# x^T and the first weight piece in shared transfers, and causal attention on two pairs of heads at a time

## The chip, the cores and the metric

The program runs on one NeuronCore of a Trainium2 chip. The metric is the device time of one execution in microseconds (us), from repeated runs of the same program; lower is better. Engines are named as the profile names them: PE is TensorE (PEld its weight loads), DVE is VectorE, ACT is ScalarE, POOL is GpSimd, SP is SyncE, which only starts DMA transfers here.

## What is computed

One layer of a decoder trunk on 256 tokens of width 1024, all in float32. The normed input goes through one projection `w_in`, whose columns feed four token mixers and their gates; the mixers are projected, gated, summed, projected once more, and a SwiGLU FFN follows. The part that matters here:

```python
h = rmsnorm(x, norm_mix)
proj = h @ w_in                       # m_z, m_xbc, m_dt, b_qkv, c_qkv, c_f, d_q, d_kv, gate_logits
y_a = mamba2_branch(...)              # A: state space scan, 8 heads
y_b = moba_attention(...)             # B: causal attention, 8 heads of 64, bias by distance
y_c = forgetting_attention(...)       # C: causal attention, 8 heads of 64, cumulative forget gates
y_d = sliding_window_attention(...)   # D: window 128, 8 query heads on 2 key heads, sinks
merged = sum(sigmoid(gate_i) * (y_i @ w_branch_i))
x = x + merged @ w_out
x = x + (silu(h2 @ w_ffn_gate) * (h2 @ w_ffn_up)) @ w_ffn_down       # h2 = rmsnorm(x, norm_ffn)
out = rmsnorm(x, norm_final)
```

With 256 tokens every attention branch is, for each head, a lower triangle of 256 by 256: 128 x 128 scores for the first half of the queries, 128 x 256 for the second.

## The kernel before, in words

**Precision.** A float32 product is made of three fast products: each operand is split into a rounded high part and the rest (`hi` and `lo`), and PE computes hi*hi, hi*lo and lo*hi. ACT makes the high parts (L331), DVE the low parts (L339).

**The weight stream.** The weights come from HBM in pieces of 1 MB, in the order of `stream()`, through three raw buffers (`fetch`, L323), all issued by SP. A piece is asked for when the low part of the piece three places ahead of it is done. The in-projection pieces come first (`xbc0`, `xbc1`, `n0`, `qkB0`, `vB0` and so on), then for the branches in the order A, B, D, C four gate pieces and two branch pieces each (PE groups `pg` at L989 and `pb`), then the out-projection `wo`, the FFN's `gu` and `dn`.

**The head.** The first piece is not fetched like the others. x^T (x transposed, 1 MB in two tiles `xT0`, `xT1`) and the piece `xbc0` (1 MB) come in six chunks of the 8 blocks of 128 rows, one transfer of x^T and one of the weights per chunk, at L395 and L397: 12 transfers, 11 of them from SP and the first of the weights from POOL, with the constants `chan` (the norm weights) between them on SP (L399). For each chunk ACT scales x^T into the high part of `xx` (L431) and makes the weights' high part (L432), DVE the two low parts (L434, L436), and PE adds the chunk's products (L440, six matmuls of 256 columns per block of 128 rows, 48 in all). Every later projection reads `xx`. Eight matmuls on constants (L424) run on PE before the first chunk. Behind the head, `xbc1` and `n0` follow on PE with no other work between; the norm's factor r comes later, from x itself (`xn`).

**Attention, woven in.** All other work of the mixers is written as generators (`att_pair`, `ssd_pair`, `conv` and others) that yield a `Need` of estimated engine time and of buffers. The `Weaver` holds clocks of PE, DVE and ACT, which are estimates, and between groups of projection matmuls (`wv.tick`) runs those stages whose inputs it takes to be ready and whose buffers are free. The order of all instructions on each engine is thus fixed when the program is built. What a stage needs before it is put on PE is (L764 and around):

```python
yield Need(pe=680, att=2)      # two PSUM banks of the five of tag att
```

One call of `att_pair` handles one pair of heads: the scores (`s`, L764 and L766, operands of 64 rows, one head in the upper and one in the lower half of PE's array), then on DVE the bias, negation and row minimum (L777, L779), on ACT the exponential (L783, L784), on DVE the division by the row sums (L801, L802), on PE six transposes (`pt`, L809), on ACT the copy (L815), on PE the products with the values (`y`, in `pv`, L685 and L687, outputs of 64 columns), and the split of y into parts. There are four pairs in each of B, C and D. The state space branch ends in `pv` too (`ya`). Rows of the bias tables come by POOL's DMA queue (`rows2`, L584).

Of the kernel before, what the change touches and what calls it, by code (L numbers as in the profile page):

```python
# [199 lines left out]
def hybrid_block_kernel(ctx: ExitStack, tc: tile.TileContext, A, out):  # L200
# [28 lines left out]

    def acc(name, shape=(128, 512)):  # L230
# [80 lines left out]
    for n in names:  # L311
# [72 lines left out]
    act.activation(early, early, AF.Exp)  # L384
    chan = const("chan", [128, 64])
    rows = const("rows", [128, 32])
# [41 lines left out]
    hb, lb, wb = (cut(t, 8, 256) for t in (h0, l0, w0))  # L428
    for a, b in chunks:
        for k in range(a, b):  # L430
            act.activation(xx(k)[:, 0, :], xT[k // 4][:, k % 4, :], AF.Copy, scale=nm_mix[:, k : k + 1])  # L431
        act.activation(hb[:, a:b, :], wb[:, a:b, :], AF.Copy)  # L432
        for k in range(a, b):
            dve.scalar_tensor_tensor(xx(k)[:, 1, :], xT[k // 4][:, k % 4, :], nm_mix[:, k : k + 1],  # L434
                                     xx(k)[:, 0, :].bitcast(F32), ALU.mult, ALU.subtract)
        dve.tensor_tensor(lb[:, a:b, :], wb[:, a:b, :], hb[:, a:b, :].bitcast(F32), ALU.subtract)  # L436
# [316 lines left out]
    def att_pair(br, j, heads, load_rows, q, k, vs, addend, sinks=None):  # L753
        yield Need(rows=1)
        rw = load_rows()
        yield Need()
        yield Need(pe=680, att=2)
        if j == 0:
            new_y(br)
        sts = []  # L760
        hs = [slice(64 * i, 64 * i + 64) for i in range(2)]
        ss = [att("s%s%d" % (br, heads[i]), [128, 384]) for i in range(2)]
        for i in range(2):
            pe.matmul(ss[i][:, 0:128], q[hs[i], 0:128], k[hs[i], 0:128], start=True, stop=True)  # L764
        for i in range(2):
# [560 lines left out]
```

## Time and profile before

| | |
|---|---|
| time, median of 3 runs | 521.33 us (520.48 to 521.71) |
| the profiled execution: its own time, its span | 519.55 us, 517.8 us |
| PE, DVE, ACT busy in the span | 98%, 68%, 55% |
| HBM read over the span | 94.46 MB |
| mean granted TensorE clock | 0.994 of full |

A line of the profile's timeline gives the start, the time taken, the engine, the source line, and the tiles written and read. Matmuls of a stream overlap in the pipeline: what one costs is the distance from its start to the next one's, not the duration shown. A float32 matmul that is not split shows as two records.

### The profile page before, as it was taken

Reading aid. Unit: us, or ns where it says so; the run is one execution under the profiler, and the core shown is the slowest. Engines: PE = TensorE matmul, PEld = TensorE weight load, DVE = VectorE, ACT = ScalarE, POOL = GpSimd, SP = SyncE. Lnnn points to the kernel's source line nnn. Section 1 sums busy time; section 2 is a strip of 40 time slices with the busy share of each in tenths; the row PEclk is TensorE's granted clock in tenths of the full one; section 3 lists DMA queues with packets and bytes.
Section 4 is the critical chain, followed back from the end, with each engine's and each line's share of the span. In section 5 each row is a group of like instructions: output and inputs, shape, how many; then the busy total and the mean of one; then the engine's idle time right before and its main releaser. Section 6 shows DMA issues by size and latency. Waiting matters only on the chain.

```text
span 517.8 us, 7989 instructions
## 1 busy us (share of the span) xinstructions
PE 507.6 (98%) x3106; PEld 444.1 (86%) x3106; DVE 350.6 (68%) x658; ACT 284.1 (55%) x511; POOL 29.7 (6%) x61
## 2 busy tenths in 40 slices
PE   7999999999999999999999999999999999999995
PEld 6998998987897778888888899998888888888884
DVE  4577778898896947547386494688676676673435
ACT  6667464567575863443444363876655655543412
POOL 2008110012110000000000000000000000000001
PEclk8999999999999999999999999999999999999998
DMA  7974464465355244727537283355545555585302
GB/s 230 388 277 173 162 217 150 156 217 192 137 177 183 82 164 162 250 92 280 191 128 278 89 332 148 97 229 177 219 173 172 215 184 169 210 313 181 144 0 82
DMA packets 17122, 96.06 MB, mean 186 GB/s; under 512 B 2235, under 2 KB 3563, under 8 KB 6844
## 3 DMA queue, kind: packets, MB, share of 16 engines
q1 hardware_dynamic: 15660, 91.15, 48.8%
q0 software_dynamic: 1424, 4.41, 3.1%
q8 instruction: 24, 0.39, 0.3%
q14 instruction: 14, 0.11, 0.1%
HBM read 94.46 MB, written 1.09 MB: 185 GB/s over the span
## 4 chain that ended last, share of the span: by engine, by line
PE 95%; issue 2%; DMA 1%; ACT 1%; DVE 1%; SPq 0%; POOL 0%; POOLq 0%; ACTq 0%; DVEq 0%
PE pg L989 17%; PE gu L260 13%; PE pd L1186 11%; PE pb L250 8%; PE gu L262 7%; PE pvC L989 2%; PE pvB L989 2%; PE qkC L252 2%; PE po L250 1%; PE gu L250 1%; PE gu L253 1%; PE po L253 1%; PE gu L252 1%; PE qkC L250 1%; PE po L252 1%
## 5 line engine op out<-in xcount | busy, mean ns | idle before, releaser
L260 PE MATMUL gu<-x3x,hi_gu 128*128 128x512 f32 x288 | 72.1, 392 | 0.0
L989 PE MATMUL pg<-hi_g,xx 128*128 128x512 f32 x256 | 64.3, 393 | 0.0
L260 PEld LDWEIGHTS gu<-x3x,hi_gu 128*128 128x128 f32 x288 | 51.8, 189 | 9.3
L989 PEld LDWEIGHTS pg<-hi_g,xx 128*128 128x128 f32 x256 | 47.4, 188 | 11.1 <-issue 1.5
L339 DVE TENSOR_TENSOR lo_gu<-raw_gu,hi_gu 128x1024 fp32r<-128x1024 f32 x44 | 53.2, 1216 | 1.4 <-ACT hi_gu L331 1.4
L331 ACT ACTIVATE hi_g<-raw_g 128x1024 fp32r<-128x1024 f32 x32 | 32.9, 1053 | 29.0 <-DMA raw_g<-in_w_dram 14.2
L331 ACT ACTIVATE hi_gu<-raw_gu 128x1024 fp32r<-128x1024 f32 x44 | 45.6, 1051 | 1.5 <-PE gu L253 1.5
L1186 PE MATMUL pd<-hi_dn,aa 128*128 128x512 f32 (+1 forms) x176 | 46.2, 384 | 0.0
L339 DVE TENSOR_TENSOR lo_g<-raw_g,hi_g 128x1024 fp32r<-128x1024 f32 x32 | 38.1, 1219 | 8.8 <-ACT hi_g L331 8.8
L262 PEld LDWEIGHTS gu<-x3x,lo_gu 128*128 128x128 f32 x288 | 39.3, 190 | 2.8
L339 DVE TENSOR_TENSOR lo_dn<-raw_dn,hi_dn 128x1024 fp32r<-128x1024 f32 x22 | 26.1, 1220 | 21.6 <-ACT hi_dn L331 21.5
L262 PE MATMUL gu<-x3x,lo_gu 128*128 128x256 f32 x288 | 40.2, 282 | 0.0
L1186 PEld LDWEIGHTS pd<-hi_dn,aa 128*128 128x128 f32 x176 | 32.6, 188 | 6.5
L331 ACT ACTIVATE hi_dn<-raw_dn 128x1024 fp32r<-128x1024 f32 x22 | 22.4, 1052 | 25.3 <-PE pd L1186 25.3
L1128 DVE TENSOR_TENSOR gs<-gu,ge 128x256 f32<-128x256 f32 x36 | 15.3, 424 | 30.7 <-ACT ge L1127 30.6
L989 PE MATMUL pg<-lo_g,xx 128*128 128x512 f32 x128 | 34.3, 389 | 0.0
L1127 ACT ACTIVATE ge<-gu 128x256 f32<-128x256 f32 x36 | 13.5, 374 | 27.5 <-PE gu L262 27.3
L989 PEld LDWEIGHTS pg<-lo_g,xx 128*128 128x128 f32 x128 | 24.0, 188 | 5.1
L1186 PE MATMUL pd<-lo_dn,aa 128*128 128x512 f32 (+1 forms) x88 | 26.7, 384 | 0.0
L339 DVE TENSOR_TENSOR lo_wb<-raw_wb,hi_wb 128x1024 fp32r<-128x1024 f32 x16 | 19.3, 1220 | 9.3 <-ACT hi_wb L331 9.3
L913 ACT ACTIVATE gate<-pg,r1h 128x512 f32<-128x512 f32 x16 | 11.0, 687 | 25.7 <-PE pg L989 25.7
L929 DVE SCALAR_TENSOR_TENSOR gp<-gate,pb 128x512 f32<-128x512 f32 x12 | 8.2, 687 | 21.2 <-PE pb L250 20.9
(326 smaller groups left out, 1140.5 us busy)
## 6 DMA issues: line engine op xcount, KB each, us to landing
raw_gu<-in_w_dram SPq DMA_DIRECT2D x22, 1024.0 KB, 4.8
raw_g<-in_w_dram SPq DMA_DIRECT2D x16, 1024.0 KB, 4.8
raw_dn<-in_w_dram SPq DMA_DIRECT2D x11, 1024.0 KB, 4.8
raw_wb<-in_w_dram SPq DMA_DIRECT2D x8, 1024.0 KB, 4.9
raw_qkB<-in_w_dram SPq DMA_DIRECT2D x4, 1024.0 KB, 5.0
raw_qkC<-in_w_dram SPq DMA_DIRECT2D x4, 1024.0 KB, 4.9
raw_wo<-in_w_dram SPq DMA_DIRECT2D x4, 1024.0 KB, 4.8
raw_vB<-in_w_dram SPq DMA_DIRECT2D x2, 1024.0 KB, 8.8
```

Of the source, the lines that this page charges most:

```text
L250: pe.matmul(o, l, r, start=start, stop=stop)
L252: pe.matmul(o, l, r[:, 0, :], start=start, stop=False)
L253: pe.matmul(o, l, r[:, 1, :], start=False, stop=stop)
L260: pe.matmul(o, wh(k), x(k), start=start and i == 0, stop=False)
L262: pe.matmul(o[:, 0, :], wl(k), x(k)[:, 0, :], start=False, stop=stop and i == n - 1)
L331: act.activation(parts[name][0][:, s], raws[name][:, s], AF.Copy)
L339: dve.tensor_tensor(lo[:, s], raws[name][:, s], hi[:, s].bitcast(F32), ALU.subtract)
L913: act.activation(gates[b, t][:, 512 * nh : 512 * nh + 512], p, AF.Tanh, scale=r1h[:, t : t + 1])
L989: pe.matmul(pg[t], l, r, start=kh == 0 and i == 0, stop=kh == 1 and i == len(terms) - 1)
L1127: act.activation(e[:, j, :], p[j][:, 1, :], AF.Copy)
L1128: dve.tensor_tensor(s[:, j, :], p[j][:, 0, :], e[:, j, :], ALU.add)
L1186: pe.matmul(o, l, r, start=start and j == 0, stop=stop and j == len(terms) - 1)
```

## The change

Two independent edits. First, x^T and the weights of `xbc0` lie side by side in one array in HBM (`head`: per block of 128 rows, 256 columns of x^T, then 256 of weights), which the host builds; they come into four tiles `hd` in five transfers, of which ACT's queue issues the second and SP the others. `chan` moves from SP to ACT's queue, POOL issues no part of the head, and the raw buffer that `xbc0` had is free from the start. Second, `att_pair` becomes `att_quad`, which handles two pairs of heads: the scores of both pairs in a row, then DVE and ACT work pair by pair, transposes pair by pair, then the products with the values of both pairs in a row. A quad reserves its buffers `pp`, `sm` and `pt` for four heads (`hold`), and asks for four of the five PSUM banks of tag `att` at its start. Which instructions there are hardly changes; their order does.

```diff
     chan = const("chan", [128, 64])
+    act.dma_start(chan, A["chan"])
...
-    xT = [slot("xT%d" % i) for i in range(2)]
-    w0 = wp.tile([128, WMAX], F32, tag="raw", name="raw_xbc0", bufs=3)
-    raws["xbc0"] = w0
-    chunks = ((0, 1), (1, 2), (2, 4), (4, 6), (6, 7), (7, 8))
+    hd = [slot("hd%d" % i, (128, 2, 2, 256)) for i in range(4)]
+    chunks = ((0, 1), (1, 2), (2, 4), (4, 6), (6, 8))
     for a, b in chunks:
-        nc.sync.dma_start(xT[a // 4][:, a % 4 : (b - 1) % 4 + 1, :], A["xT"][:, a:b, :])
-        src = bass.AP(tensor=A["w"].tensor, offset=woff["xbc0"] + 256 * a, ap=[[2048, 128], [1, 256 * (b - a)]])
-        (nc.sync if a else pool).dma_start(w0[:, 256 * a : 256 * b], src)
-        if a == 0:
-            nc.sync.dma_start(chan, A["chan"])
+        (act if a == 1 else nc.sync).dma_start(hd[a // 2][:, a % 2 : (b - 1) % 2 + 1, :, :], A["head"][:, a:b, :, :])
+    act.activation(early, early, AF.Exp)
...
-    def att_pair(br, j, heads, load_rows, q, k, vs, addend, sinks=None):
-        yield Need(rows=1)
-        rw = load_rows()
+    def att_quad(br, pairs, addend, sinks=None):
+        rws = []
+        for _, _, load_rows, _, _, _ in pairs:
+            yield Need(rows=1)
+            rws.append(load_rows())
         yield Need()
-        yield Need(pe=680, att=2)
-        if j == 0:
+        yield Need(pe=1360, att=4, pp=4, sm=4)
+        hold(pp=4, sm=4)
+        if pairs[0][0] == 0:
             new_y(br)
...
+        for ss, (_, _, _, q, k, _) in zip(sss, pairs):
+            for i in range(2):
+                pe.matmul(ss[i][:, 0:128], q[hs[i], 0:128], k[hs[i], 0:128], start=True, stop=True)
+        for ss, (_, _, _, q, k, _) in zip(sss, pairs):
+            for i in range(2):
+                pe.matmul(ss[i][:, 128:384], q[hs[i], 128:256], k[hs[i], 0:256], start=True, stop=True)
...
+        yield Need(pe=1300, att=2)
+        ys = [att("y%s%d" % (br, p[0]), [128, 256]) for p in pairs]
+        for y, sts, p in zip(ys, stss, pairs):
+            pv(y, p[5], sts)
+            rel(pt=2)
...
-    for j in range(4):
-        wv.later(lambda j=j: moba_pair(j), ["qkB%d" % j, "vB0", "vB1", "erow"], True)
+    for js in ((0, 1), (2, 3)):
+        wv.later(lambda js=js: moba_quad(js), ["qkB%d" % j for j in js] + ["vB0", "vB1", "erow"], True)
...
-    a["w"] = np.concatenate([pk(ps[n]) for n in stream()])
+    a["w"] = np.concatenate([pk(ps[n]) for n in stream()[1:]])
+    a["head"] = np.stack([a["xT"], pk(ps[stream()[0]]).reshape(128, 8, 256)], 2)
```

The queue of SP at the program's start, before (`xT` and `raw_xbc0` are the head, sizes in partitions x elements; `raw_xbc1` and `raw_n0`, the next two pieces, stand right behind these rows):

```order
L395 DMA xT0_81<-in_xT_dram 128x256
L399 DMA chan_79<-in_chan_dram 128x64
L395 DMA xT0_81<-in_xT_dram 128x256
L397 DMA raw_xbc0_83<-in_w_dram 128x256
L395 DMA xT0_81<-in_xT_dram 128x512
L397 DMA raw_xbc0_83<-in_w_dram 128x512
L395 DMA xT1_82<-in_xT_dram 128x512
L397 DMA raw_xbc0_83<-in_w_dram 128x512
L395 DMA xT1_82<-in_xT_dram 128x256
L397 DMA raw_xbc0_83<-in_w_dram 128x256
L395 DMA xT1_82<-in_xT_dram 128x256
L397 DMA raw_xbc0_83<-in_w_dram 128x256
```

and with the change:

```order
L399 DMA hd0_81<-in_head_dram 128x512
L399 DMA hd1_82<-in_head_dram 128x1024
L399 DMA hd2_83<-in_head_dram 128x1024
L399 DMA hd3_84<-in_head_dram 128x1024
L328 DMA raw_xbc1_91<-in_w_dram 128x512 x4
L328 DMA raw_n0_96<-in_w_dram 128x2176
```

Twelve transfers stood ahead of `raw_xbc1` on SP, now four; `chan` and the second half of `hd0` stand on ACT's queue, ahead of all its other work.

On PE, the values' products of the first pair of branch B stood before next to the scores of the second, between the projection pieces `xbc3` and `z0`:

```order
L250 MATMUL xbc3_763<-xx3_119,lo_xbc3_609 128x256 x2
L685 MATMUL yB0_850<-ptsB0_846,vB_565 64x256
L685 MATMUL yB0_850<-ptsB1_848,vB_565 64x256
L687 MATMUL yB0_850<-ptsB0_846,vB_565 64x128
L687 MATMUL yB0_850<-ptsB1_848,vB_565 64x128
L764 MATMUL sB2_858<-qkB0_438 128x128
L764 MATMUL sB3_859<-qkB0_438 128x128
L766 MATMUL sB2_858<-qkB0_438 128x256
L766 MATMUL sB3_859<-qkB0_438 128x256
L252 MATMUL z0_864<-xx0_116,hi_z0_697 128x256
```

With the change the scores of all four heads stand in that place, and the products of both pairs follow later, in the middle of `qD0`:

```order
L255 MATMUL xbc3_721<-xx3_113,lo_xbc3_601 128x256 x2
L772 MATMUL sB0_803<-qkB0_430 128x128
L772 MATMUL sB1_804<-qkB0_430 128x128
L772 MATMUL sB2_805<-qkB0_430 128x128
L772 MATMUL sB3_806<-qkB0_430 128x128
L775 MATMUL sB0_803<-qkB0_430 128x256
L775 MATMUL sB1_804<-qkB0_430 128x256
L775 MATMUL sB2_805<-qkB0_430 128x256
L775 MATMUL sB3_806<-qkB0_430 128x256
L257 MATMUL z0_815<-xx0_110,hi_z0_679 128x256
```

The scores of the first pair moved back from `qkB1` to this place, and 12 runs of scores in the program became 6.

The end of the attention work moved too. Before, the last products of branch C (`yC3`) were on PE ahead of the first branch projection `pb000`. With the change the last quad begins only ahead of the third branch's projection, and its end stands 24 gate matmuls ahead of the matmuls that read it:

```order
L689 MATMUL yC3_3017<-ptsC6_3012,vC_1474 64x128
L689 MATMUL yC3_3017<-ptsC7_3014,vC_1474 64x128
L1014 MATMUL pg211_2995<-hi_g211_2927,xx2_112 128x512 x4
L1014 MATMUL pg211_2995<-hi_g211_2927,xx3_113 128x512 x4
L1014 MATMUL pg211_2995<-lo_g211_2928,xx2_112 128x512 x2
L1014 MATMUL pg211_2995<-lo_g211_2928,xx3_113 128x512 x2
L1014 MATMUL pg210_2960<-hi_g211_2927,xx2_112 128x512 x4
L1014 MATMUL pg210_2960<-hi_g211_2927,xx3_113 128x512 x4
L1014 MATMUL pg210_2960<-lo_g211_2928,xx2_112 128x512 x2
L1014 MATMUL pg210_2960<-lo_g211_2928,xx3_113 128x512 x2
L255 MATMUL pb200_3064<-hi_wb20_2976,yC0_2113 128x512 x4
L255 MATMUL pb200_3064<-hi_wb20_2976,yC1_2114 128x512 x4
```

So the attention of branches C and D now lies partly between the gate and branch projections, where before there was none.

## Rows read from the trace of the kernel before

**Rows 1.** The page: busy time of PE, and the chain by engine.
```profile
PE 507.6 (98%) x3106; PEld 444.1 (86%) x3106; DVE 350.6 (68%) x658; ACT 284.1 (55%) x511; POOL 29.7 (6%) x61
...
PE 95%; issue 2%; DMA 1%; ACT 1%; DVE 1%; SPq 0%; POOL 0%; POOLq 0%; ACTq 0%; DVEq 0%
```

**Rows 2.** Waits of PE from 27 us on: total us, times, longest.
```profile
PE yB L685 <- ACT ptsB L815: 0.9, 1, 0.9
```

**Rows 3.** Timeline, all engines, first 21 us: start, us, engine, line, operation.
```profile
4.21 0.51 ACT L431 ACTIVATE xx<-xT,chan 128x256 fp32r<-128x256 f32 x1 [1.99 <-DMA chan<-in_chan_dram]
...
5.08 1.12 PE L440 MATMUL xbc<-xx,hi_xbc 128*128 128x256 f32 x4 [0.22 <-ACT hi_xbc L432]
...
7.78 0.91 ACT L431 ACTIVATE xx<-xT,chan 128x256 fp32r<-128x256 f32 x2 [2.05 <-DMA xT<-in_xT_dram]
...
8.60 0.61 ACT L432 ACTIVATE hi_xbc<-raw_xbc 128x512 fp32r<-128x512 f32 x1
...
9.26 2.01 PE L440 MATMUL xbc<-xx,hi_xbc 128*128 128x256 f32 x8 [2.10 <-ACT hi_xbc L432]
...
15.18 0.28 PE L252 MATMUL xbc<-xx,hi_xbc 128*128 128x256 f32 x1
...
15.30 0.28 PE L253 MATMUL xbc<-xx,hi_xbc 128*128 128x256 f32 x1
...
18.41 2.12 ACT L331 ACTIVATE hi_n<-raw_n 128x1088 fp32r<-128x1088 f32 x2 [2.15 <-DMA raw_n<-in_w_dram]
...
20.94 2.17 PE L250 MATMUL n<-hi_n,xx 128*128 128x272 f32 x16
```

**Rows 4.** Windows of 0.5 us: engines' busy us, then granted clock, DMA share, GB/s.
```profile
9.50:10.00 0.50, 0.50 (x3) 0.50 (x3) 0.43 (x2) 0.50 (x2) 0.00 (x0) 0.50 0.89 279
...
13.00:13.50 0.50, 0.50 (x6) 0.50 (x5) 0.50 (x2) 0.50 (x1) 0.00 (x0) 1.00 1.09 301
```

**Rows 5.** Windows of 5 us, the same columns (PE, PEld, DVE, ACT, POOL).
```profile
0.00:5.00 5.00, 3.78 (x16) 3.49 (x16) 0.47 (x3) 2.27 (x5) 2.69 (x10) 1.00 0.55 145
5.00:10.00 5.00, 2.82 (x15) 2.62 (x16) 2.88 (x8) 2.70 (x8) 0.00 (x0) 0.94 0.92 278
10.00:15.00 5.00, 5.00 (x33) 5.00 (x33) 4.24 (x9) 3.77 (x9) 0.00 (x0) 0.72 0.96 306
15.00:20.00 5.00, 5.00 (x44) 5.00 (x44) 1.83 (x3) 2.54 (x4) 0.00 (x0) 1.00 1.01 419
```

**Rows 6.** Timeline of PE: scores of one pair alone between projection matmuls.
```profile
50.79 0.49 PE L764 MATMUL sB<-qkB 64*128 64x128 f32 x4
...
51.65 0.38 PE L252 MATMUL qkB<-xx,hi_qkB 128*128 128x256 f32 x1
51.87 0.28 PE L253 MATMUL qkB<-xx,hi_qkB 128*128 128x256 f32 x1
```

**Rows 7.** Timeline of PE: values' products of one pair alone.
```profile
105.74 0.65 PE L685 MATMUL ya<-dw,xc 128*64 128x256 f32 x4
...
106.54 0.39 PE L252 MATMUL qkC<-xx,hi_qkC 128*128 128x256 f32 x1
```

**Rows 8.** Timeline of PE: values' products of two pairs that happen to be neighbours.
```profile
149.34 0.65 PE L685 MATMUL yD<-ptsD,vD 128*64 128x256 f32 x4
...
150.79 0.39 PE L252 MATMUL qkC<-xx,hi_qkC 128*128 128x256 f32 x1
```

**Rows 9.** Timeline of PE: transposes of one pair alone.
```profile
77.37 0.82 PE L809 MATMUL ptB<-ident,pB 128*128 128x128 f32 x6
77.94 0.36 PE L252 MATMUL qkB<-xx,hi_qkB 128*128 128x256 f32 x1
```

**Rows 10.** Timeline of PE: transposes of one pair with another pair's scores behind.
```profile
127.52 0.82 PE L809 MATMUL ptB<-ident,pB 128*128 128x128 f32 x6
...
129.12 0.39 PE L252 MATMUL qkC<-xx,hi_qkC 128*128 128x256 f32 x1
```

**Rows 11.** Windows: attention's stretch before, and gates and branches; columns as above.
```profile
50.79:192.44 141.65, 140.75 (x1046) 121.60 (x1045) 115.94 (x317) 87.47 (x209) 13.77 (x23) 1.00 0.50 171
192.44:300.00 107.56, 107.56 (x480) 89.17 (x479) 62.47 (x64) 47.17 (x53) 0.00 (x0) 1.00 0.51 185
```

More of the change, by code (lines that the diff above doesn't have):

```diff
@@ L228, in rel, with hold @@
             wv.free[t] += n
+    def hold(**tags):
+        for t, n in tags.items():
+            wv.free[t] -= n
     def acc(name, shape=(128, 512)):
@@ L310, in hybrid_block_kernel @@
     o_ = 0
-    for n in names:
+    for n in names[1:]:
         woff[n] = o_
@@ L383, in hybrid_block_kernel @@
     dve.memset(ones, 1.0)
-    act.activation(early, early, AF.Exp)
     chan = const("chan", [128, 64])
+    act.dma_start(chan, A["chan"])
     rows = const("rows", [128, 32])
@@ L759, in att_pair @@
             new_y(br)
-        sts = []
         hs = [slice(64 * i, 64 * i + 64) for i in range(2)]
[L762 to L765, printed above, removed]
-            pe.matmul(ss[i][:, 128:384], q[hs[i], 128:256], k[hs[i], 0:256], start=True, stop=True)
-        pp, sms, exs = [], [], []
-        fox = br == "C"
-        yield Need(dve=2520 if fox else 1200, act=1300, sp=2, pp=2, ff=2 * fox, nm=2, sm=2, rs=2)
@@ L792, in att_pair @@
-        rel(rows=1)
-        yield Need(dve=1100, rs=2)
-        for i in range(2):
-            p, sm = pp[i], sms[i]
-            if sinks is not None:
-                dve.tensor_tensor(sm, sm, exs[i], ALU.add)
-                rel(rs=1)
-            r = work("r%s%d" % (br, heads[i]), [128, 2], "rs")
-            dve.reciprocal(r, sm)
-            dve.tensor_scalar(p[:, 128:384], p[:, 128:384], r[:, 1:2], None, ALU.mult)
-            dve.tensor_scalar(p[:, 0:128], p[:, 0:128], r[:, 0:1], None, ALU.mult)
-            rel(rs=1, sm=1)
@@ new lines, in att_quad @@
+        stss = []
+        yield Need(pt=4)
+        hold(pt=4)
+        for (j, heads, _, _, _, _), pp, sms, exs in zip(pairs, pps, smss, exss):
+            yield Need(dve=1100, rs=2)
+            for i in range(2):
+                p, sm = pp[i], sms[i]
+                if sinks is not None:
+                    dve.tensor_tensor(sm, sm, exs[i], ALU.add)
+                    rel(rs=1)
+                r = work("r%s%d" % (br, heads[i]), [128, 2], "rs")
+                dve.reciprocal(r, sm)
+                dve.tensor_scalar(p[:, 128:384], p[:, 128:384], r[:, 1:2], None, ALU.mult)
+                dve.tensor_scalar(p[:, 0:128], p[:, 0:128], r[:, 0:1], None, ALU.mult)
+                rel(rs=1, sm=1)
+            pts, sts = [], []
+            yield Need(pe=660, att=2)
+            for i in range(2):
+                pt = att("pt%s%d" % (br, heads[i]), [128, 384])
+                for c in range(3):
+                    pe.transpose(pt[:, tok(c)], pp[i][:, tok(c)], ident)
+                rel(pp=1)
+                pts.append(pt)
+            yield Need(act=830)
+            rel(pt=2)
+            for i in range(2):
+                st = work("pts%s%d" % (br, heads[i]), [128, 384], "pt")
+                act.activation(st, pts[i], AF.Copy)
+                sts.append(st)
+            rel(att=2)
+            stss.append(sts)
@@ new lines, in att_quad @@
+        yield Need(pe=1300, att=2)
+        ys = [att("y%s%d" % (br, p[0]), [128, 256]) for p in pairs]
+        for y, sts, p in zip(ys, stss, pairs):
+            pv(y, p[5], sts)
+            rel(pt=2)
+        for y, (j, *_) in zip(ys, pairs):
+            yield Need(act=360)
+            act.activation(yh(br, j), y, AF.Copy)
+        for y, (j, *_) in zip(ys, pairs):
+            yield Need(dve=340)
+            dve.tensor_tensor(yl(br, j), y, yh(br, j).bitcast(F32), ALU.subtract)
+            rel(att=1)
+            wv.done.add("y%s%d" % (br, j))
```

120 lines of the change are left out of this document (54 added, 66 removed).

## The prediction

> **What bounds the kernel now.** I read the page first, then PE's waits, then the timeline and the windows of the head, then PE's timeline at the attention work. The page says that PE is busy for 507.6 of 517.8 us and that 95% of the chain that ended last is PE [rows 1]. From 27 us on PE waits for another engine once, for 0.9 us [rows 2]. So the time after the head is the sum of what PE is given, and two things can shorten it: a head that hands over to `xbc1` sooner, or fewer PE microseconds for the same matmuls. The change tries one of each. The profiled execution took 519.55 us, 1.78 below the median of the runs and 0.9 below the lowest of them; I make the sum against 519.55 and add 1.78 at the end. A difference of 0.2% (1.0 us) is about what a measurement of this kernel can tell from none.
>
> In the head the reader is to see three losses [rows 3]. PE starts on the first chunk at 5.08 us. After the second chunk it has nothing: ACT's next scaling waits 2.05 us for a transfer of x^T, starts at 7.78, and PE goes on at 9.26 after 2.10 us idle. Then the granted clock, full until then, stands at half; it is 0.50 from 9.5 and back at 1.00 at 13.0 [rows 4]. At half speed from 9.5 to nearly 13 us PE does in 3.4 us the work of 1.7. The 48 matmuls of the head end at 15.18, where `xbc1` begins; at the pace of 0.12 us (15.18 to 15.30) they need only 5.8 us [rows 3]. From there to 27 us PE has no gap.
>
> **The head, with the change.** What sets it is when the bytes come. The windows give 145, 278, 306 and 419 GB/s in the first four stretches of 5 us [rows 5], so 0.73 MB had moved by 5 us, 2.12 by 10, 3.65 by 15 and 5.74 by 20. Suppose the same curve, and put the change's transfers on it in their order: `chan`, the first two blocks and the small constants are 0.64 MB, there at about 4.7 us; the three transfers of two blocks (0.52 MB each) are complete at 1.16, 1.69 and 2.21 MB, that is at 6.6, 8.5 and 10.3 us. For two blocks ACT takes 0.91 + 0.61 = 1.52 us [rows 3], so the weights' high parts are there at 8.1, 10.0 and 11.8; DVE's parts are made while PE does the high-part products. The last 12 matmuls then take 1.44 us: the head ends at 13.3 instead of 15.18, a gain of 1.9 us. The gaps of PE on the way are about 1.2, 0.5 and 0.4 us, shorter than the 2.1 us ahead of which stood the fall of the clock, so I take the clock to stay.
>
> If the bytes come faster, ACT is the bound: from 4.2 us, eight blocks at half of 1.52, plus some 0.2 us for the two single ones, end at 10.5, PE at 11.9, and the gain is 3.2 us. For this speaks that the same 16 engines moved 419 GB/s once transfers of a megabyte were under way, against 278 with a share of 0.92 when x^T and weights came in runs of 1 to 2 KB [rows 5]; the merged chunks have runs of 2 to 4 KB. At the low end, the clock falls all the same and takes back 1.7, which leaves 0.2. I take **2.4 us**, between the two ends that keep the clock, nearer to the curve that was measured.
>
> Here a rule speaks against the second queue. The trace shows a DMA share of 0.92 to 0.96 from 5 to 15 us with SP's queue nearly alone [rows 5], so there is little left for another queue to fill. The Trainium skill says so outright (DMA: Bandwidth & Descriptors, Rules for kernel authors): spreading transfers over SP, ACT and GpSimd does not raise bandwidth, since all use the same 16 engines, and saves only the sequencer's issue time. By that rule alone the head would gain 1.9, by the larger runs up to 3.2; the same page's advice to coalesce small transfers points to the second.
>
> The gain must survive the next stage. On the same curve `xbc1` is complete at 3.26 MB (13.7 us), and its four pieces are used over 5.8 us from 13.3 on; `n0` is complete at 4.37 MB, 16.7 us. Before, ACT got `n0` at 18.41 and PE used it at 20.94 [rows 3]; with the change PE is at `n0` at about 18.5 to 19. Even if `n0` came no sooner than before, its first half would be split at 18.41 + 1.06 = 19.5, and 1.4 of the 2.4 us would stay. `chan` and one chunk on ACT's queue stand ahead of its table load, both over before the first chunk lands at about 4.2, so I cost them at nothing; the cover is ACT's idle 1.99 us ahead of 4.21 [rows 3].
>
> **Attention, with the change.** PE's matmuls are the same; their neighbours are not. One pair's scores alone keep the projection matmuls away for 0.86 us (50.79 to 51.65), and the first projection matmul behind takes 0.22 until the next one starts instead of 0.12 [rows 6]. One pair's products with the values take 0.80 (105.74 to 106.54) [rows 7], but two pairs that stand together take 1.45 (149.34 to 150.79) [rows 8]: the second costs 0.65, so 0.15 is the price of entering that kind of matmul. For scores no row shows two pairs together. They have as many records of the same numbers of columns as the products, so I take 0.65 for the second pair too and 0.21 saved; the ends are nothing and 0.21. The terms:
>
> - 12 runs of scores become 6: 6 x 0.21 = 1.3 us less.
> - 14 runs of products with values (the four of the state space branch among them; two runs held two pairs) become 10: 4 x 0.15 = 0.6 less.
> - Transposes and scores that were neighbours at four places took 1.60 (127.52 to 129.12) [rows 10], though alone they take 0.57 [rows 9] and 0.86 [rows 6]; no such neighbours are left: 4 x 0.17 = 0.7 less.
> - The places where projections are broken off go from 30 to 34, as neighbours are parted: 4 x 0.10 = 0.4 more.
> - The 0.9 us that PE waited for ACT's copy of transposes [rows 2]: there 24 projection matmuls lay between transposes and products; for that quad it is now 48. Elsewhere the distance is as it was. I take 0.8 of it as gone; at the ends it is all back, or 1.6 with the stutter behind it.
>
> Sum: 1.3 + 0.6 + 0.7 - 0.4 + 0.8 = **3.0 us** less, between about 0 and 3.8.
>
> DVE's and ACT's work in a quad is the same, and more spread out. Before, DVE was busy 115.94 of 141.65 us from the first scores to the last products, then only 62.47 of 107.56 [rows 11]; three of the six quads now end in the second stretch. The one late end that could be forced is the last quad, and 24 gate matmuls stand between its products and their readers, ample for two copies and two subtractions. POOL's queue loses one transfer at the start, and its table rows stand in an order that puts both rows of a quad together; DVE meets them tens of microseconds later.
>
> In all 2.4 + 3.0 = 5.4 us: 514.15 for the profiled execution, and against the median 521.33 - 5.4 = **515.9 us**.
>
> **The rivals.**
>
> *One half pays nothing.* Either the clock falls in the head once more and 1.7 of its 2.4 are lost (517.6), or the attention gains are eaten by new waits of the size of the one seen, three of 0.9 and a little (518.9). For the first speaks that the clock did fall when PE had idled for 2.10 of 2.4 us; against it, that the gaps will be half as long. Chance 0.18.
>
> *The change does not do what it says.* The first chunk is twice the bytes, so it lands later, the last chunk with it, `n0` stays where it was, and the fused runs save nothing because what costs is the step from one matmul to another, which happens as often. Then 521.3, within 1 us. Rows 8 speak against the second part. Chance 0.08.
>
> *A quad starves the weights' low parts, and it is slower.* DVE works in order. A quad puts the reduction of four heads on it in one go, where two stood; the second pair's share is what the planner books, 1.2 us in B and D and 2.5 in C, and the low part of a coming weight piece may stand behind it. If all six quads show on PE, that is 2 x 1.2 + 2 x 1.2 + 2 x 2.5 = 9.8 us, and 521.33 - 5.4 + 9.8 = 525.7. It decides where a low part is needed less than that after it is made. In its favour is DVE at 82% in that stretch [rows 11]; against it, that parts are made one to two pieces ahead, a piece being 48 matmuls or 5.8 us, and that PE waited once in the whole stretch [rows 2]. Chance 0.10.
>
> **How the numbers follow.** The forecast has 0.64, the rivals 0.18, 0.08 and 0.10. Faster by more than 0.2% are the first two, 0.82; the third is within 0.2%, 0.08; the last slower, 0.10. The low end takes both good bounds, 3.2 and 3.8: 514.3, less 0.8 for the spread of a median: 513.5. The high end is the rival without a gain in attention, 518.9. Outside lie the other two rivals and a little of the forecast.
>
> **What would show it.** Right: `xbc1` begins on PE near 12.8 us, no window of half clock between 9 and 13 us, the scores of a quad take about 1.50 us from the first to the next projection matmul and its products 1.45, and PE has no wait over 1 us behind the head. Wrong in the head: a gap of PE over 2 us or a half clock behind it, or `n0` split later than 17.5. Wrong in attention: waits of PE for DVE's low parts, or scores of a quad at 1.7. A span above 517 us would make the prediction wrong as a whole.

## The result and the profile after

The changed kernel takes 514.37 us, median of 4 runs (514.25 to 517.55), against 521.29 (520.48 to 521.71) of the kernel before beside it: a ratio of 0.9884, 95% interval 0.9844 to 0.9924, 6.9 us less. Three runs lie within 0.2 us of each other; the fourth, 517.55, is the profiled one, and the one thing that the trace can show of what sets it apart is in the head, below.

The page of the changed kernel (busy time, share of the span, instructions; then the chain that ended last):

```profile
PE 505.6 (98%) x3106; PEld 444.1 (86%) x3106; DVE 349.7 (68%) x657; ACT 283.7 (55%) x510; POOL 29.9 (6%) x60
...
PE 96%; DMA 1%; issue 1%; DVE 0%; ACT 0%; POOL 0%; ACTq 0%; POOLq 0%
```

PE's waits in the changed kernel (total us, times, longest):

```profile
PE xbc L442 <- ACT hi_xbc L434: 2.9, 2, 2.3
PE warm L425 <- DVE cumu L388: 1.1, 1, 1.1
```

The bound is the same as before [rows 1], and the wait for `ptsB` [rows 2] is gone; PE waits for no engine behind the head.

**Attention.** Timeline of PE in the changed kernel at the scores of one quad, and at the products of another:

```profile
65.76 0.71 PE L772 MATMUL sB<-qkB 64*128 64x128 f32 x8
66.31 1.03 PE L775 MATMUL sB<-qkB 64*128 64x256 f32 x8
67.27 0.39 PE L257 MATMUL z<-xx,hi_z 128*128 128x256 f32 x1
67.50 0.28 PE L258 MATMUL z<-xx,hi_z 128*128 128x256 f32 x1
...
95.53 0.65 PE L687 MATMUL yB<-ptsB,vB 128*64 128x256 f32 x4
96.01 0.39 PE L689 MATMUL yB<-ptsB,vB 128*64 128x128 f32 x4
96.23 0.60 PE L687 MATMUL yB<-ptsB,vB 128*64 128x256 f32 x4
96.66 0.39 PE L689 MATMUL yB<-ptsB,vB 128*64 128x128 f32 x4
96.98 0.39 PE L257 MATMUL qD<-xx,hi_qD 128*128 128x256 f32 x1
```

Two pairs' scores take 1.51 us (65.76 to 67.27), where one pair took 0.86 [rows 6]; two pairs' products take 1.45 (95.53 to 96.98), as [rows 8] had it. All six quads show 1.51 and 1.45.

**The head.** Timeline of the changed kernel's head, all engines:

```profile
1.17 0.45 ACTq L399 DMA_DIRECT2D hd<-in_head_dram  x1
...
4.43 0.51 ACT L433 ACTIVATE xx<-hd,chan 128x256 fp32r<-128x256 f32 x1 [1.28 <-DMA chan<-in_chan_dram]
...
5.30 0.74 PE L442 MATMUL xbc<-xx,hi_xbc 128*128 128x256 f32 x4 [0.56 <-ACT hi_xbc L434]
...
7.79 0.51 ACT L433 ACTIVATE xx<-hd,chan 128x256 fp32r<-128x256 f32 x1 [2.54 <-DMA hd<-in_head_dram]
...
8.65 1.22 PE L442 MATMUL xbc<-xx,hi_xbc 128*128 128x256 f32 x4 [2.31 <-ACT hi_xbc L434]
...
15.95 2.12 ACT L336 ACTIVATE hi_n<-raw_n 128x1088 fp32r<-128x1088 f32 x2 [1.31 <-DMA raw_n<-in_w_dram]
...
16.45 0.28 PE L257 MATMUL xbc<-xx,hi_xbc 128*128 128x256 f32 x1
...
22.21 2.17 PE L255 MATMUL n<-hi_n,xx 128*128 128x272 f32 x16
```

Half-microsecond windows of the same stretch (busy us and counts of PE, PEld, DVE, ACT, POOL; granted clock, DMA share, GB/s):

```profile
6.00:6.50 0.50, 0.35 (x3) 0.14 (x2) 0.00 (x0) 0.00 (x0) 0.00 (x0) 1.00 1.09 433
6.50:7.00 0.50, 0.00 (x0) 0.00 (x0) 0.00 (x0) 0.00 (x0) 0.00 (x0) 1.00 2.07 290
7.00:7.50 0.50, 0.00 (x0) 0.00 (x0) 0.00 (x0) 0.00 (x0) 0.00 (x0) 1.00 1.35 107
7.50:8.00 0.50, 0.00 (x0) 0.00 (x0) 0.00 (x0) 0.21 (x1) 0.00 (x0) 0.90 0.20 74
8.00:8.50 0.50, 0.00 (x0) 0.00 (x0) 0.17 (x1) 0.50 (x2) 0.00 (x0) 0.50 0.58 158
8.50:9.00 0.50, 0.35 (x1) 0.35 (x2) 0.50 (x2) 0.50 (x3) 0.00 (x0) 0.50 0.78 279
...
15.00:15.50 0.50, 0.50 (x7) 0.50 (x5) 0.50 (x2) 0.00 (x0) 0.00 (x0) 1.00 1.00 411
```

In this execution the head became worse. From 3.5 to 6.5 us the transfers ran at 365 to 433 GB/s, where the kernel before had 278 from 5 to 10 [rows 5], but from 6.5 to 8.5 us the rate fell, to 74 GB/s at the lowest; the second chunk, the one on ACT's queue, came at 7.8. PE idled 2.31 us, the clock went to half at 7.9 and came back at 14.7, and PE reached `n` at 22.21, 1.27 later than before [rows 3]. From `n` to the end it needed 493.55 us of the span, before 496.83 (20.94 to 517.77). The three other runs are some 3.2 us shorter; their spans have mean granted clocks of 0.997 to 0.999 against 0.991. They have no trace, so that they kept the full clock in the head is likely and not shown. So two things had to be settled: what each half is worth by itself, and what makes the hole in the transfers.

### The profile page after: what moved, and what is told of

The parts are those of the page before. It is cut to its first block, busy times and chain, and to the rows that moved or that the text cites. A ratio compares the mean times of both kernels' runs of the same rounds, so it can differ in the third digit from the quotient of the medians.

```text
span 515.8 us, 7963 instructions
## 1 busy us (share of the span) xinstructions
PE 505.6 (98%) x3106; PEld 444.1 (86%) x3106; DVE 349.7 (68%) x657; ACT 283.7 (55%) x510; POOL 29.9 (6%) x60
## 4 chain that ended last, share of the span: by engine, by line
PE 96%; DMA 1%; issue 1%; DVE 0%; ACT 0%; POOL 0%; ACTq 0%; POOLq 0%
PE pg L1014 17%; PE gu L265 13%; PE pd L1211 11%; PE pb L255 9%; PE gu L267 7%; PE pvC L1014 2%; PE pvB L1014 2%; PE qkC L257 2%; PE xbc L442 2%; PE qkB L257 2%; PE qkB L255 1%; PE po L255 1%; PE gu L255 1%; PE qkC L255 1%; PE gu L258 1%; PE po L258 1%
## 5 line engine op out<-in xcount | busy, mean ns | idle before, releaser
L336 ACT ACTIVATE hi_wb<-raw_wb 128x1024 fp32r<-128x1024 f32 x16 | 16.7, 1055 | 6.8 <-PE pg L1014 6.8
```

Of the source, the lines that this page charges most:

```text
L336: act.activation(parts[name][0][:, s], raws[name][:, s], AF.Copy)
```

## The experiments

Three marks of PE describe each run: when `xbc1` starts (end of the head), when `n` starts, and how long it is from there to the first matmul of the out-projection `po`, which holds all of attention and nothing of the head. All come from PE's timeline, in us, of the one execution of each kernel that was profiled (the kernel before: the one of 519.55 us); the times are medians of all runs, with their range.

| kernel | `xbc1` | `n` | `n` to `po` | time (range, runs) | ratio to before |
|---|---|---|---|---|---|
| before | 15.18 | 20.94 | 281.36 | 521.29 (520.48 to 521.71, 4) | |
| changed | 16.45 | 22.21 | 277.42 | 514.37 (514.25 to 517.55, 4) | 0.9844 to 0.9924 |
| head alone | 13.73 | 19.49 | 280.98 | 518.41 (517.50 to 519.70, 7) | 0.9938 to 0.9971 |
| quads alone | 15.20 | 21.21 | 277.45 | 516.52 (516.00 to 517.33, 6) | 0.9905 to 0.9936 |
| one queue | 16.29 | 22.05 | 277.43 | 514.65 (514.13 to 517.37, 6) | 0.9872 to 0.9918 |
| fillers | 14.09 | 19.85 | 277.46 | 514.95 (514.72 to 516.49, 6) | 0.9877 to 0.9913 |
| POOL's queue empty | 12.69 | 18.45 | 277.44 | 513.82 (513.79 to 514.41, 5) | 0.9822 to 0.9890 |
| products apart | 13.02 | 18.78 | 278.36 | 516.70 (515.48 to 518.17, 6) | 0.9876 to 0.9943 |
| scores apart | 13.36 | 19.12 | 280.06 | 517.47 (516.58 to 519.41, 6) | 0.9893 to 0.9958 |
| twelve, two queues | 16.56 | 22.32 | 277.45 | 518.77 (517.76 to 520.43, 12) | 0.9931 to 0.9974 |
| `rows` on SP | 12.82 | 18.58 | 277.47 | 515.03 (513.81 to 515.25, 4) | 0.9845 to 0.9907 |
| halves | 12.08 | 17.84 | 277.86 | 513.77 (513.56 to 514.62, 4) | 0.9835 to 0.9886 |
| before, POOL's queue empty | 14.33 | 21.59 | 283.20 | 521.40 (519.83 to 522.79, 12) | 0.9984 to 1.0019 |
| transposes together | 13.59 | 19.34 | 277.79 | 515.02 (514.19 to 516.37, 5) | 0.9856 to 0.9907 |

One more run of the kernel with the scores apart took 1766 us; it is in the median (517.30 without it) and left out of the range. The intervals are those of the ratio to the runs of the kernel before beside each kernel (medians of 521.29, 521.00, 520.86 and 520.88). They are some 2 to 4 us wide, so differences of a microsecond or two between changed kernels can't be told from none by time. `n` to `po` is the finer measure.

### The halves of the change, each alone

Head alone: the changed head, `att_pair` as before.

```diff
-    for js in ((0, 1), (2, 3)):
-        wv.later(lambda js=js: moba_quad(js), ["qkB%d" % j for j in js] + ["vB0", "vB1", "erow"], True)
+    for j in range(4):
+        wv.later(lambda j=j: moba_pair(j), ["qkB%d" % j, "vB0", "vB1", "erow"], True)
...
```

> The head of the change with attention pair by pair as before. Theory: attention gains about 3.3 us whatever the head does, and the head gains about 3.5 us in executions in which the clock stays and loses about 1 where it falls: a median near 518, single runs from 517.5 to 521. Rival (the head is the whole gain): 514 to 515.

Quads alone: the head as before, `att_quad`.

```diff
-    hd = [slot("hd%d" % i, (128, 2, 2, 256)) for i in range(4)]
...
+    xT = [slot("xT%d" % i) for i in range(2)]
...
```

> The head as before with attention in quads. Theory: the head hands over at about 15.2 us as before, a quad's scores take 1.51 us and its products 1.45, PE waits nowhere behind the head, and the time is 3.3 us under the kernel before: 518.0. Rival (the head is the whole gain): 521.

Measured against their own runs of the kernel before (521.0): the head 2.6 us, the quads 4.5, together 6.6 to 6.9. The sum of the parts, 7.1, is nearly the whole; neither pays for the other. The quads are worth more than the 3.0 forecast and the 3.3 expected here, and `n` to `po` gives their share without the head: 281.36 less 277.45, 3.9 us, the same to 0.05 us in every kernel with unaltered quads but one (the halves, 277.86, which lose 0.4 between `n` and `qkB`, ahead of attention).

The pairs are not as even as the quads. With the same order on PE, `n` to `po` took 281.36 us in the kernel before, 280.98 with the head alone and 283.20 in the kernel before with three transfers moved (below): PE waited for `ptsB` 0.9, 0.9 and 2.7 us (1.78 and 0.89). So the quads' gain is 3.5 to 5.8 us, by the execution that they are held against.

### The late chunk

One queue: the second chunk comes from SP like the others.

```diff
-        (act if a == 1 else nc.sync).dma_start(hd[a // 2][:, a % 2 : (b - 1) % 2 + 1, :, :], A["head"][:, a:b, :, :])
+        nc.sync.dma_start(hd[a // 2][:, a % 2 : (b - 1) % 2 + 1, :, :], A["head"][:, a:b, :, :])
```

> The change, with the second chunk issued by SP like the others; chan stays on ACT's queue. Theory (that chunk came last because it stood alone on the second queue beside 1.8 MB on the first): it lands right behind the first, before 6 us, PE idles under 1.5 us in the head, the clock stays full and every run is at 514.4 or less. Rival (the engines are full and any chunk at that place lands late): a gap of 2 us or more stays, and a half clock behind it.

Timeline of ACT and PE in the head of that kernel:

```profile
4.69 0.49 ACT L433 ACTIVATE xx<-hd,chan 128x256 fp32r<-128x256 f32 x1
...
8.90 0.91 ACT L433 ACTIVATE xx<-hd,chan 128x256 fp32r<-128x256 f32 x2 [3.40 <-DMA hd<-in_head_dram]
...
10.38 1.86 PE L442 MATMUL xbc<-xx,hi_xbc 128*128 128x256 f32 x7 [2.90 <-ACT hi_xbc L434]
```

Now the second chunk is in time (4.69) and the third is 3.40 us late. The time is that of two queues, and so is the rate: 243 GB/s over the first 6.5 us with one queue, 235 with two. The Trainium skill (DMA: Bandwidth & Descriptors, Rules for kernel authors) says that spreading transfers over SP, ACT and GpSimd doesn't help bandwidth; the trace agrees. What is late in these two executions is the chunk that is due from 6.5 to 8.5 us.

Fillers: four matmuls on constants behind each of the first three chunks.

```diff
+        if a < 4:
+            for _ in range(4):
+                pe.matmul(warm, ones, ones, start=True, stop=True)
```

> The change with 4 constant matmuls on PE behind each of the first three chunks (12 of 0.21 us at full clock), two queues as in the change. Theory (the half clock comes from PE's idle time): the clock stays full in all runs, and the runs agree at 514 to 515 although the second chunk lands late. Rival (the clock falls for another reason): a half clock stays in the profile, and 12 matmuls add up to 2.5 us: 517.

ACT's scaling of the second chunk in that kernel:

```profile
6.24 0.51 ACT L433 ACTIVATE xx<-hd,chan 128x256 fp32r<-128x256 f32 x1 [1.03 <-DMA hd<-in_head_dram]
```

The clock stood at 1.00 through the head, `n` started at 19.85, and five of six runs lie within 0.7 us. But the condition of the test didn't come about: the second chunk was there at 6.2, not at 7.8, and two kernels without fillers in which it was there at 6.2 and 6.8, products apart and scores apart, kept the full clock too. So it is not shown that the fillers hold the clock. The median is 0.5 to 0.7 above the three good runs of the changed kernel, which can't be told from none.

### What makes the hole

DMA queues of the changed kernel from 5 to 9 us (packets, MB, share of the 16 engines; POOL's queue is q0, SP's q1, ACT's q10):

```profile
q1 hardware_dynamic: 241, 0.87, 57.0%
q0 software_dynamic: 94, 0.08, 36.7%
q10 hardware_dynamic: 67, 0.11, 7.0%
```

The same line of the kernel before:

```profile
q0 software_dynamic: 64, 0.02, 2.3%
```

In the trace's packet records the difference is the broadcast of `rows` (L419): its 16 packets of 1 KB took up to 1.65 us each, median 1.43, all begun between 6.6 and 8.3 us. In the kernel before they had a median of 0.05.

POOL's queue empty: `ident`, `tab` and `rows` are issued by SP behind x.

```diff
-    pool.dma_start(ident, A["ident"])
-    pool.dma_start(tab[0:32, :], A["rel_bias"])
-    pool.dma_start(rows, bass.AP(tensor=A["rows"].tensor, offset=0, ap=[[0, 128], [1, 32]]))
+    nc.sync.dma_start(ident, A["ident"])
+    nc.sync.dma_start(tab[0:32, :], A["rel_bias"])
+    nc.sync.dma_start(rows, bass.AP(tensor=A["rows"].tensor, offset=0, ap=[[0, 128], [1, 32]]))
```

> The changed kernel with the three small transfers of POOL's queue (ident, tab, rows) issued by SP behind x instead. In every run with merged chunks the windows show the rate falling from about 400 to 25 to 110 GB/s for 1.5 to 2 us between 6.5 and 8.5 us, whichever chunk is due then; between 5 and 9 us POOL's queue holds 37% of the 16 engines' time for 94 packets and 0.08 MB. Theory: these small packets make the hole; without them no window of half a us between 4 and 14 us falls under 250 GB/s, no chunk is over 1.2 us late on ACT, PE has no gap over 1 us in the head and the clock stays whole; 513.5 to 514.3 us, and no run near 517. Rival: the hole has another cause (the queue's ring, HBM itself) and POOL's packets are merely caught in it: the hole stays where it was, 514.2 to 515, with runs near 517 as before.

`rows` on SP: the last of those three edits alone.

> The changed kernel with one of POOL's three small transfers, the broadcast of rows (128 bytes to each of 128 partitions, 16 KB), issued by SP behind x; ident and tab stay with POOL. In the changed kernel's trace the 16 packets of this broadcast took 0.6 to 1.6 us each, one on every DMA engine, between 6.6 and 8.2 us, where a 4 KB packet of the chunks takes 0.16; in the kernel before the same 16 packets took 0.05 to 0.3. Theory (these packets alone make the hole): as with all three moved, 513.6 to 514.3 us, no run over 515, no gap of PE over 1 us in the head, POOL's queue under 5% of the engines' time from 5 to 9 us. Rival (ident or tab, or POOL's queue as such): the hole stays at 6.5 to 8.5 us and some runs lie over 516.

Windows of the kernel with only `rows` moved:

```profile
6.50:7.00 0.50, 0.00 (x0) 0.00 (x0) 0.23 (x1) 0.50 (x3) 0.00 (x0) 1.00 1.03 394
...
8.50:9.00 0.50, 0.50 (x5) 0.50 (x6) 0.50 (x1) 0.50 (x2) 0.00 (x0) 1.00 0.52 78
```

and its POOL queue from 5 to 9 us:

```profile
q0 software_dynamic: 64, 0.07, 4.8%
```

With `rows` gone from POOL's queue the hole at 6.5 to 8 us is gone, the head ends at 12.7 to 12.8 in both kernels, and the clock keeps. Over all traces it is the same: the six with merged chunks and `rows` on POOL's queue have the hole (25 to 78 GB/s in its lowest half microsecond), the four without don't. In that the theory holds, and `rows` is the one that counts.

What the hole costs depends on the chunk that is due in it. With products apart `rows` is on POOL's queue, and this is ACT's second chunk and the lowest window:

```profile
6.17 0.51 ACT L433 ACTIVATE xx<-hd,chan 128x256 fp32r<-128x256 f32 x1 [1.01 <-DMA hd<-in_head_dram]
```

```profile
7.50:8.00 0.50, 0.50 (x5) 0.36 (x3) 0.50 (x3) 0.50 (x2) 0.00 (x0) 1.00 0.37 45
```

The hole is there, but the chunk had landed ahead of it, as it had with the head alone, the fillers and the scores apart (ACT waited 1.0 to 1.5 us for it, and 1.06 and 1.25 with the hole gone). With products and scores apart, kernels with the changed head, the head ends at 13.02 and 13.36, 0.2 to 0.7 us later than with the hole gone; where the second chunk (changed) or the third (one queue) fell into it and the clock went to half, it ends more than 3 us later.

Where the theory was wrong: a second, shallower hole stands from 8 to 9.5 us in both (184 and 111 GB/s with the queue empty, 78 at the lowest with `rows` moved). It comes behind the last chunk and delays nothing in the head. No trace has both holes. Over the first 8 us the whole chunks come at 269 to 272 GB/s without the first hole and at 214 to 232 with it, over the first 10 us at 255 to 259 and 236 to 247. So the move puts part of the loss behind the last chunk and doesn't avoid all of it; whether both holes have one cause stays open.

In time the gain can't be told from none. With all three moved the median is 513.82 us, 7.0 under its own runs of the kernel before; the changed kernel is 6.9 under its own. What may be had is evenness: of the 18 runs of the four kernels with `rows` moved one is above 516 (transposes together, 516.37), of the ten of the changed kernel and of one queue three are. These are too few to show it. With `rows` alone three of four runs are 1 us longer than with all three moved, two over the 515 that the theory allowed, and PE had a gap of 1.01 us in the head; its profile has the microsecond in the FFN (a wait of 0.5 us of `gu` for `x3x`), far behind the edit, and why is open.

Before, POOL's queue empty: the same edit on the kernel before (POOL still issues the first chunk of the weights there).

> The kernel before with POOL's three small transfers issued by SP behind x, nothing else. Theory (there the packets of rows took 0.05 us, so they cost nothing, and the head is slow by its small runs): within 0.5 us of the kernel before, 520.3 to 521.3, a gap of PE near 2 us after the second chunk still there. Rival (POOL's queue slows any head): 518.5 to 519.5, the gap under 1 us.

521.40 us, ratio 1.0002: nothing, as the theory had it. The gap behind the second chunk is 2.7 us there. POOL's broadcast costs where it falls into the stream of merged chunks; in the old head it costs nothing that can be measured.

### Fewer transfers, longer runs?

Twelve, two queues: the quads with the old arrays, x^T from SP, the weights and `chan` from ACT (the edit against the kernel before).

```diff
-        (nc.sync if a else pool).dma_start(w0[:, 256 * a : 256 * b], src)
+        act.dma_start(w0[:, 256 * a : 256 * b], src)
```

> The quads with the head's data as before, in 12 transfers with runs of 1 to 2 KB, but from two queues from the start: x^T from SP, the weights and chan from ACT, none from POOL. Theory (the merged chunks gain by their larger runs, 145 to 278 GB/s becoming 185 to 430 in the first microseconds): the rate stays at 200 to 300 GB/s, the head as in the quads with the old head, 516.2 to 516.8. Rival (they gain because fewer and earlier issues let the data start sooner): the rate rises above 350 by 4 us and the time is that of the changed kernel, 514.3 to 515.

It doesn't decide what it was made for. ACT scales the first chunk only at 8.38 us, since its seven issues take until 6.94 and its table load of 1.28 us stands behind them; PE idles 4.37 us and `n` comes at 22.32. What it shows is the price of issues on an engine that has work to do.

Halves: POOL's queue empty, and each chunk as two transfers from the same array, in runs of 1 KB.

```diff
-        (act if a == 1 else nc.sync).dma_start(hd[a // 2][:, a % 2 : (b - 1) % 2 + 1, :, :], A["head"][:, a:b, :, :])
+        for i in range(2):
+            (act if a == 1 else nc.sync).dma_start(hd[a // 2][:, a % 2 : (b - 1) % 2 + 1, i, :], A["head"][:, a:b, i, :])
```

> The version with POOL's queue empty, but every chunk of the head as two transfers, x^T's half and the weights' half, so ten transfers with runs of 1 KB out of the same array and from the same queues. Theory (the merged transfers gain by their longer runs and by being fewer): the rate from 3.5 to 7 us falls from 370 to 430 GB/s to 200 to 300 as in the kernel before, the last chunk comes 2 to 3 us later, n starts on PE at 20 to 21.5 instead of 18.45, 515.5 to 517. Rival (only the empty queue of POOL and the order of the issues count): n at 18.5 to 19, 513.8 to 514.3.

Its windows, and then its timeline of ACT:

```profile
3.50:4.00 0.50, 0.50 (x4) 0.50 (x3) 0.00 (x0) 0.50 (x2) 0.00 (x0) 1.00 0.63 197
...
4.50:5.00 0.50, 0.50 (x3) 0.25 (x3) 0.25 (x2) 0.50 (x2) 0.00 (x0) 1.00 0.83 252
```

```profile
3.53 0.49 ACT L434 ACTIVATE xx<-hd,chan 128x256 fp32r<-128x256 f32 x1
4.34 0.42 ACT L435 ACTIVATE hi_xbc<-hd 128x256 fp32r<-128x256 f32 x1 [0.32 <-DMA hd<-in_head_dram]
4.66 0.49 ACT L434 ACTIVATE xx<-hd,chan 128x256 fp32r<-128x256 f32 x1
5.75 0.42 ACT L435 ACTIVATE hi_xbc<-hd 128x256 fp32r<-128x256 f32 x1 [0.59 <-DMA hd<-in_head_dram]
```

The rate does fall, to 197 to 371 GB/s from 3.5 to 7 us where the whole chunks had 369 to 430, so fewer transfers with longer runs are faster; but the head is not later, it is the earliest of all, with `xbc1` at 12.08. ACT scales the first half chunk at 3.53 instead of 4.21 (there `chan` came last, here ACT came from its table load and waited for no transfer), and from then on it is hardly kept waiting. The theory that the merging makes the gain falls. Even so this head moves more bytes early than the old one: 238 GB/s over the first 8 us, against 188 in the kernel before and 164 with its three small transfers moved. What is left between the two is the order of the issues (`chan` and a chunk off SP's queue), ten transfers for twelve, and the one array; these were not taken apart, so why the head gains stays open.

### What fusing is worth

Products apart: in a quad, the products of each pair by themselves.

```diff
-        yield Need(pe=1300, att=2)
-        ys = [att("y%s%d" % (br, p[0]), [128, 256]) for p in pairs]
...
+            yield Need(pe=650, att=1)
+            ys.append(att("y%s%d" % (br, p[0]), [128, 256]))
```

> The changed kernel with the products with the values pair by pair again, each where its pair's copies are ready, the rest of the quad as it is. Runs of products go from 10 to 15, four of them now directly ahead of a quad's scores. Theory (entering a kind of matmul costs 0.15 each time): 5 x 0.15 = 0.75 us more, and up to 0.17 for each of the four new neighbours, so 0.8 to 1.4 us over the changed kernel, 515.1 to 515.9, by the distance from PE's start of n to the end of the span 0.8 to 1.4 more than the 493.3 to 493.6 seen there. Rival (what the quads gain is the vanished waits and their stutter, the fusing itself gives nothing): within 0.3 of the changed kernel, 514.3 to 514.7.

`n` to `po` is 0.9 us more, inside the theory's 0.8 to 1.4, and so is `n` to the end, the theory's own measure, with 1.4 (494.92 us, the changed kernel 493.55); no wait came back. The median time is 2.3 us more, over the 515.9 expected, which the profile doesn't explain: it is of the lowest run, 515.48, and the intervals of the two kernels overlap.

Scores apart: the two pairs' scores in two runs.

```diff
+            if n:
+                yield Need(pe=680)
+            ss = [att("s%s%d" % (br, h), [128, 384]) for h in heads]
```

> The changed kernel with the scores of a quad's two pairs in two separate runs, the rest as it is. Runs of scores go from 6 to 12; by the planner's doing runs of products fall from 10 to 8. Theory (0.21 for each run of scores, 0.15 for each run of products): 6 x 0.21 - 2 x 0.15 = 1.0 us over the changed kernel, 515.4, and 1.0 more from PE's start of n to the end. Rival (only the waits count): within 0.3 of the changed kernel.

2.6 us more to `po`, and no wait behind the head on PE's list. Each run of scores takes 0.85 again, 12 of them for 6 x 1.51: 1.1 us. Another 1.0 comes from the order that the planner then makes: a run of products of four pairs, two of B and two of the state space, takes 3.72 us for the 2.75 of its parts. PE and DVE in that run, which begins at 101.46:

```profile
102.97 0.90 PE L687 MATMUL ya<-dw,xc 128*64 128x256 f32 x3
```

```profile
102.36 1.97 DVE L715 TENSOR_TENSOR dw<-dex,cbs 128x384 f32<-128x384 f32 x4 [4.24 <-PE yB L689]
```

The state space's products read `dw`, and DVE makes it only from 102.36 to 104.33, when the products of B ahead have freed its buffers; from 102.97 on PE takes 2.21 us for two pairs' products, 1.30 of the 2.75. That it waits there tile by tile is inferred, as each wait would be too short for its list. The last 0.5 is a run of transposes, products and scores, 3.35 us for the 2.88 of its parts. The rival falls: where PE's list shows no wait, parting the runs costs what they cost.

Transposes together, on the version with POOL's queue empty: both pairs' transposes in one run.

```diff
-            yield Need(pe=660, att=2)
...
+        yield Need(pe=1320, att=4)
```

> The version with POOL's queue empty, and the transposes of a quad's two pairs in one run as well. Runs of transposes go from 12 to 6, runs of products by the planner's doing from 10 to 8 (one of them of four pairs). Theory (each run has a price, and each place where projections are broken off 0.10): 8 fewer places, 0.8 us, and 2 x 0.15 for the products, up to 0.2 for each pair of transposes: from PE's start of n to the start of po 1.1 to 2 us less than the 277.44 seen, 512 to 512.7 us. Rival (the longer run makes its readers late: ACT copies four tiles in one go, and the products of four pairs wait for them, as in the kernel with the scores apart, where such a run took 3.72 instead of 2.75): no gain or up to 1 us lost, 513.8 to 514.8.

Timeline of PE at such a run:

```profile
88.41 1.47 PE L831 MATMUL ptB<-ident,pB 128*128 128x128 f32 x12
89.64 0.36 PE L257 MATMUL qD<-xx,hi_qD 128*128 128x256 f32 x1
```

A miss. Twelve transposes take 1.23 us, not less than twice 0.57, so no price of entering shows for them; they are 128 by 128, like the projections beside them. A run of products of four pairs came about again and took 3.78. `n` to `po` is 0.35 longer, as the rival had it, but not for its reason: ACT's copies were done at 94.3, 4.2 us before that run began, and what came late was `dw` again, which DVE made from 99.42 to 101.38.

## Why the prediction was right

The time lies in the range, 1.5 us below the number, and the sign is right. The attention half came by the mechanism named; the head's number came close without its mechanism, which is luck. By its steps:

- **What bounds the kernel:** right. PE sets the end in all kernels here.
- **Attention, 3.0 us:** the mechanism right, the sum too small; measured 3.9. The runs of scores, 1.3, are 1.26 (12 x 0.86 less 6 x 1.51); the value taken for the second pair's scores, 0.65, was exact. The products, 0.6, are confirmed by the kernel that parts them. Transposes beside scores, 0.7, were 0.8. The mis-sized term is the wait: I took 0.8 for its 0.9 us and the stutter, and all of it went, 0.9 and 0.7 (a run of products had 1.17 us instead of 0.80, one of products and scores 2.02 instead of 1.66). The upper end of that term, 1.6, was the truth, and the upper end of the sum, 3.8, nearly so. But the term has no fixed size: by the two other traces with pairs it is 1.3 and 3.4. The sum's lower end, "about 0", is lower than the terms' own ends give (3.0 less 1.3 and 0.8 is 0.9).
- **The head, 2.4 us:** about right in size, 2.6 with the head alone, but not by the reason given. In single traces with the whole chunks the head ends between 1.3 us later (changed) and 2.5 earlier (POOL's queue empty) than before. The rule on queues that was set against it held. The byte curve did not: the rate was higher than before and had a hole. The longer runs, which I named as the cause of the better end, raise the rate and are not what the head gains by. With the hole out of the way the head ends at 12.7, near the 12.8 I looked for. One reading was wrong as well: the clock of the kernel before was not "full until then". The record of the clock begins at 5.95 us there, and after the four matmuls that begin at 5.08 [rows 3] the next start at 6.04, so they stand 0.24 us apart, half of the full pace of 0.12:

  ```profile
  6.04 0.41 PE L440 MATMUL xbc<-xx,lo_xbc 128*128 128x256 f32 x2
  ```

- **The rival "the clock falls again", 517.6:** it is what happened in the profiled run, 517.55. I had it as another way for the kernel to be; it is another way for one execution to go, and the median hides it. That the numbers agree is chance: the rival left 0.7 of the head's gain and 3.0 in attention, the trace lost 1.3 in the head, won 3.9 up to `po` and lost 0.7 behind it.
- **The rival "quads starve the low parts", 525.7:** didn't happen. No wait for DVE behind the head shows in the changed kernel; the one that a trace with quads has, 0.5 us for `x3x`, is in the FFN.
- **The signs:** `xbc1` was at 16.45 and not near 12.8. Scores of a quad at 1.50, products at 1.45 and no wait behind the head were as named. The half clock behind a gap over 2 us, named as wrong in the head, was there too, but a sign read from one execution tells of that execution.

## What to carry to other kernels

Put matmuls of one kind (row halves, column halves) side by side: on PE the price is paid on entering the kind, here 0.21 us for scores and 0.15 for products, and what a second group costs can be read from a row where two already stand together. Twelve transposes in a run saved nothing. Merging pays only as long as what the run reads is made in time; a run of four pairs lost a microsecond to DVE's `dw`. When transfers at a kernel's start get faster, look at the small ones that now fall among them: with a 16 KB broadcast on another queue came a hole in the stream that cost a few tenths of a microsecond, or 3 us where a chunk was due in it, while the choice of queue and the length of runs showed no difference in time.

## What the runs showed of the hardware

- The 16 packets of a broadcast of 128 bytes to 128 partitions took a median of 1.43 us each when they met the merged chunks' stream of some 400 GB/s (1.19 to 1.63 in five more traces), and 0.05 in a stream of some 280 [rows 5] or, with twelve transfers from two queues, of 205 to 369. The fast streams are also the ones with packets of 4 KB from SP, so rate and packet size are not taken apart. With SP issuing the broadcast behind x the stream had no hole up to 8 us. Why is not shown.
- A gap of PE of some 2 us did not always bring the half clock. It followed gaps of 2.10 (before), 1.97 (quads alone), 2.31 (changed) and 2.90 us (one queue), but not one of 2.67, in the kernel before with three transfers moved:

```profile
9.13 1.21 PE L440 MATMUL xbc<-xx,hi_xbc 128*128 128x256 f32 x8 [2.67 <-ACT hi_xbc L432]
```

  The granted clock is 1.00 there, and the eight matmuls take 1.21 us, where they took 2.01 behind the shorter gap before [rows 3]. So the length of a gap alone doesn't tell what the clock will do.
- A clock of 1.00 in the windows can be an absence of records. In the kernel with the transposes together the windows say 1.00 throughout the head, but the trace's record of the clock begins at 10.34 us, and up to there the pace is about half of that with POOL's queue empty. First that kernel's timeline, then the other's:

```profile
6.13 0.63 PE L442 MATMUL xbc<-xx,lo_xbc 128*128 128x256 f32 x2
...
8.40 1.95 PE L442 MATMUL xbc<-xx,hi_xbc 128*128 128x256 f32 x8
...
10.72 1.11 PE L442 MATMUL xbc<-xx,hi_xbc 128*128 128x256 f32 x8
```

```profile
5.81 0.40 PE L442 MATMUL xbc<-xx,lo_xbc 128*128 128x256 f32 x2
...
8.28 1.21 PE L442 MATMUL xbc<-xx,hi_xbc 128*128 128x256 f32 x8 [0.27 <-ACT hi_xbc L434]
...
9.81 1.12 PE L442 MATMUL xbc<-xx,hi_xbc 128*128 128x256 f32 x8
```

  Eight matmuls take 1.95 us and, later in the same head, 1.11. That head ended 0.9 us later for it (13.59 against 12.69), with waits for chunks that agree to 0.05 us. The head alone ran at half the pace up to 10.7 in the same way. At a kernel's start the pace of the matmuls tells the clock, the column may not.
